# A two-layer encoder trunk: 128-row rotated queries in the attention of layer 0, and the expert selection on 16-bit positions, spread over 55 blocks

## The chip, the cores and the metric

The kernel runs on one core of a Trainium2 chip. The metric is the device time of one execution in microseconds (us); the median of three timed runs of the kernel before is given below. A profiled execution of the same kernel gives the rows.

The engines are TensorE (PE, with its weight loads PEld), VectorE (DVE), ScalarE (ACT), GpSimd (POOL) and SyncE (SP), which issues the DMAs here. Each works through its own instructions in order; semaphores tie them together.

## The reference

256 tokens of width 1024 go through two layers in float32. Each layer is an attention followed by a mixer called PEER, both with a residual and a LayerNorm. The attention of layer 0 is a latent attention: a head's query and key have a content part of 128 and a rotary part of 64, and the rotary key is shared by all heads.

```python
q = einsum('bsr,rhd->bshd', rmsnorm(cq), w_uq)         # 8 heads, 128 + 64
q_nope, q_rope = split(q, [128], axis=-1)
q_rope = apply_rope(q_rope, cos, sin)                  # 64 wide
k_rope = apply_rope(k_rope, cos, sin)                  # one for all heads
q, k = concat([q_nope, q_rope]), concat([k_nope, k_rope])
s = where(key_chunk <= query_chunk, q @ k.T * 192**-0.5, -inf)
o = softmax(s) @ v
```

PEER picks 16 of 16384 experts for each token and head, from two lists of 128 scores:

```python
v1, i1 = top_k(s1, 16);  v2, i2 = top_k(s2, 16)
cand     = v1[..., :, None] + v2[..., None, :]         # 16 x 16 sums
cand_idx = i1[..., :, None] * 128 + i2[..., None, :]   # their experts
best, pos = top_k(cand, 16)
expert = take_along_axis(cand_idx, pos)                # the lookup
gate   = softmax(best)
y = sum over (head, expert) of gelu(x . w_down[expert]) * gate * w_up[expert]
```

## The kernel before

**Weights and products.** All weights come as blocks of 128 x 1024 float32, `raw`, that SP's queue loads in the order of use (`Stream`). ScalarE rounds a block to `hi` (L83) and VectorE makes the rest `lo = raw - hi` (L85); activations are held as such pairs too. `mm3` then does every product as three matmuls, hi by hi, hi by lo and lo by hi (L211). At most three blocks are split ahead of the one in use (`AHEAD`).

**Layer 0's attention.** `mla` makes the normed queries and keys. The rotary queries `qr` hold two heads per tile, head 2i in partitions 0 to 63 and head 2i + 1 in 64 to 127; `rope` writes them with one addition over all 128 partitions (L447). The rotary key `kr` stands twice, in both halves. In `scores` each of two query tiles does a content matmul over 128 rows and a rotary one over 64 (the rows of one head, `qk`, L628 to 630), in float32, followed by mask and maximum on VectorE, the exponential on ScalarE and a division on VectorE. `output` transposes the probabilities (`pt`) and multiplies by the values (`o`). One head's scores are computed ahead of the head whose output is taken.

**PEER.** It doesn't gather. It computes the dot products of all tokens with all 16384 experts and weights them by a mostly empty matrix of gates. First come 16 blocks of queries (`pq`) and the scores (`ps`). Then come 128 blocks of `w_down`: a block is 24 matmuls of 128 x 256 into half a PSUM tile `d`. After each pair of blocks ScalarE applies Gelu and the result is kept in the arena `A`. At last 128 blocks of `w_up` (`y`) multiply `A`.

**The selection.** During the `w_down` blocks the generator `choose` is advanced, `STEPS` calls per block, 2 and 1 alternately. It has 68 steps. For each half of the tokens (t = 0, 1) it first takes the top 16 of each of 16 lists, then forms the 50 sums that can be among the best 16 (`cand`, and on GpSimd their expert numbers `cell`), takes their top 16 with positions `pos`, and looks the numbers up. The lookup of a head is a one-hot and a sum: VectorE compares a counter of 50 cells with the 16 positions (L791, 800 elements a partition, float32, position by position, the cells inmost), GpSimd multiplies by the cells in place (L793), and VectorE adds up over the cells one head later (L796). Behind both halves come the gates, the transposes `gT`, and the split of an expert number into `i1t` and `i2t`.

**Placing.** When the generator has ended (at block 44), 64 groups of four tokens follow. For a token `prepare` makes one-hots of 128 elements in 16-bit floats: `V` on GpSimd (L837), `U` with the gate on VectorE (L838), its rest `L` on ScalarE (L839). `place` multiplies them with eight matmuls into a PSUM tile `G` and folds `G` into `A`. Two groups go with every pair of blocks, and one when fewer than that suffice to end at block 120. The one-hots of two groups are held at a time.

**What sets the order.** The program is written with a tile scheduler: a pass over it with modelled times decides the order of instructions on every engine. So an instruction of the generator need not stand beside the block in whose turn it was written. `STEPS` and the tiles that an instruction needs decide how early it can stand.

Of the kernel before, what the change touches and what calls it, by code (L numbers as in the profile page):

```python
# [12 lines left out]
F16 = mybir.dt.float16  # L13
U32 = mybir.dt.uint32
AF = mybir.ActivationFunctionType
ALU = mybir.AluOpType
AX = mybir.AxisListType

P = 128
T = 256  # L20
# [4 lines left out]
HEADS = 8  # L25
NKEYS = 128
TOPK = 16
# [13 lines left out]
CELLS = sum(SEG)  # L41
STAGGER = 4
STEPS = (2, 1)
FIRST = 4
# [102 lines left out]
def tile_trunk(ctx: ExitStack, tc: tile.TileContext, ins, out: bass.AP):  # L147
    nc = tc.nc
# [3 lines left out]
    const = pool("const", 1)  # L152
# [29 lines left out]
    gr = const.tile([P, T], F32, tag="gr", name="gr")  # L182
    iota16 = const.tile([P, P], F16, tag="iota16", name="iota16")
    arena = big.tile([P, 32768], F32, tag="arena", name="arena")
    A = arena.rearrange("p (b t) -> p b t", t=T)

    make_identity(nc, ident)
    nc.gpsimd.iota(iota, pattern=[[1, P]], base=0, channel_multiplier=0, allow_small_or_imprecise_dtypes=True)
    nc.vector.tensor_copy(iota16, iota)
    nc.vector.memset(ones, 1.0)  # L190
    nc.vector.memset(mhalf, -0.5)
# [243 lines left out]

    def rope(o, p, cos, sin, half, tmp):
        n = p.shape[1]
        xs = tmp()[:, :n, :]
        t1 = tmp()[:, :n, :]
        for q in range(0, P, 2 * half):  # L440
            nc.scalar.copy(xs[q : q + half], p[q + half : q + 2 * half])
            nc.scalar.copy(xs[q + half : q + 2 * half], p[q : q + half])
        cb = cos[:, None, :].to_broadcast([P, n, T])
        sb = sin[:, None, :].to_broadcast([P, n, T])
        nc.vector.tensor_tensor(t1, p, cb, op=ALU.mult)
        nc.gpsimd.tensor_tensor(xs, xs, sb, op=ALU.mult)
        nc.vector.tensor_tensor(o, t1, xs, op=ALU.add)  # L447

# [62 lines left out]
    def mla():  # L511
# [7 lines left out]
        rms = ar.take(2, 2)  # L519
        qn, qr = ar.take(HEADS, T), ar.take(HEADS // 2, T)  # L520
        kn, kr = ar.take(HEADS, T), ar.take(T)
        v = ar.take(2, D)
        oh, ol = xh, xl

        hp = [py(i, f"h{i}") for i in range(3)]
# [73 lines left out]
        for h in range(0, HEADS // 2, 2):  # L599
            p = ps(f"qr{h}")  # L600
            pv = p.rearrange("p (j t) -> p j t", t=T)
            up(pv[:, 0, :], 0, 3)
            up(pv[:, 1, :], 0, 3)
            rope(qr[:, h : h + 2, :], pv, cos, sin, 32, tmp)
        rq = inverse_rms(0, 3, 0)
# [22 lines left out]
        def qk(h):  # L628
            r = slice((h % 2) * 64, (h % 2) * 64 + 64)
            return [(qn[:, h, :], kn[:, h, :]), (qr[r, h // 2, :], kr[r, :])]  # L630

# [84 lines left out]
    def peer(li):  # L716
# [11 lines left out]
        pos = [ar.take(HEADS, TOPK).bitcast(U32) for _ in range(2)]  # L728
        posf = [ar.take(HEADS, TOPK) for _ in range(2)]
        exp_ = [ar.take(HEADS, TOPK) for _ in range(2)]  # L730
        hot = ar.ring(2, TOPK, CELLS)
        scr = ar.ring(2, NKEYS)
        qrow = [arena[:, half - (2 - t) * 512 : half - (1 - t) * 512] for t in range(2)]
# [31 lines left out]
        def choose():  # L765
            for t in range(2):
# [15 lines left out]
                for h in range(HEADS):  # L782
                    top16(best[t][:, h, :], pos[t][:, h, :], cand[t][:, h, :], scr()[:, :CELLS])
                    if h % 2:
                        yield
                nc.vector.tensor_copy(posf[t], pos[t])
                held = None
                for h in range(HEADS + 1):
                    if h < HEADS:
                        o = hot()  # L790
                        nc.vector.tensor_tensor(o, iota[:, None, :CELLS].to_broadcast([P, TOPK, CELLS]),  # L791
                                                posf[t][:, h, :, None].to_broadcast([P, TOPK, CELLS]), op=ALU.is_equal)
                        nc.gpsimd.tensor_tensor(o, o, cell[t][:, h, None, :].to_broadcast([P, TOPK, CELLS]), op=ALU.mult)  # L793
                        yield
# [199 lines left out]
```

## Time and profile before

| | |
|---|---|
| median of 3 runs | 1901.88 us (1901.61 to 1902.59) |
| profiled execution, its span | 1900.2 us, 1898.4 us |
| busy: TensorE, its weight loads | 98%, 88% of the span |
| busy: VectorE, ScalarE, GpSimd | 71%, 56%, 30% of the span |

A row of a group of instructions names its line, engine and operation, then what is written and what is read by the program's names; most tiles of the selection are called `arena`, the big buffer that they are cut from. In a timeline the first number is the start from the beginning of the span and the second the length, both in us. Instructions of one engine overlap at their edges, so the step from one start to the next says more than the length. The granted clock of TensorE, where a view has it, is a share of full speed.

### The profile page before, as it was taken

To read this page: it belongs to the slowest core of one execution; us is meant where nothing else is said; L and a number is where in the kernel's file an instruction comes from. 1 tells how busy PE (TensorE), PEld (TensorE's weight loads), DVE (VectorE), ACT (ScalarE), POOL (GpSimd) and SP (SyncE) were. 2 spreads that over 40 slices of the span, in tenths; PEclk is the share of its full clock that TensorE was granted. 3 is DMA by queue.
4 is the path that set the end of the run, shared out by engine and by line. 5 is a ranking of instruction groups with operands and counts; after the bars stand their busy time and mean duration, and the time that the engine had idled before them with its cause. 6 is when DMAs were issued, how large, how long until landed. Compare 5 with 4: busy or idle time off the path is not lost.

```text
span 1898.4 us, 33300 instructions
## 1 busy us (share of the span) xinstructions
PE 1858.9 (98%) x12482; PEld 1673.4 (88%) x12482; DVE 1356.6 (71%) x2771; ACT 1058.3 (56%) x1837; POOL 565.4 (30%) x648
## 2 busy tenths in 40 slices
PE   8999999999999999999999999999999999999998
PEld 7789999999998888888798799999999988888886
DVE  5579998788766555555668689997887765555555
ACT  6554446777655444444466444558777554444443
POOL 2001346999620000000033003359998400000000
PEclk9999999999999999999999999999999999999999
DMA  6365455444557655555654554554444565555553
GB/s 231 116 217 167 147 176 179 156 156 157 167 172 231 189 189 188 190 188 189 209 167 151 181 160 159 178 189 146 156 157 162 172 228 190 188 191 188 190 187 113
DMA packets 93763, 335.51 MB, mean 177 GB/s; under 512 B 10401, under 2 KB 11425, under 8 KB 93601
## 3 DMA queue, kind: packets, MB, share of 16 engines
q1 hardware_dynamic: 93312, 332.87, 53.3%
q8 instruction: 97, 1.59, 0.3%
q14 instruction: 66, 0.53, 0.1%
q10 hardware_dynamic: 288, 0.52, 0.1%
HBM read 329.16 MB, written 4.19 MB: 176 GB/s over the span
## 4 chain that ended last, share of the span: by engine, by line
PE 85%; DVE 9%; issue 2%; POOL 1%; ACT 1%; DMA 1%; SPq 0%; DVEq 0%; POOLq 0%; ACTq 0%
PE y L211 40%; PE d L211 31%; PE pq L211 4%; PE G L211 3%; DVE lo L85 3%; PE v L211 1%; PE q L211 1%; POOL VU L837 1%; PE s L211 1%; DVE arena L791 1%; DVE arena L796 1%; PE ps L211 1%; PE qw L211 1%; PE qi L211 1%; PE h L211 1%
## 5 line engine op out<-in xcount | busy, mean ns | idle before, releaser
L85 DVE TENSOR_TENSOR lo<-raw,hi 128x1024 fp32r<-128x1024 f32 x587 | 745.4, 1272 | 340.4 <-ACT hi L83 338.6
L83 ACT CAST hi<-raw 128x1024 fp32r<-128x1024 f32 x592 | 619.3, 1048 | 600.1 <-PE y L211 224.3
L211 PE MATMUL d<-xh,lo 128*128 128x256 f32 x2048 | 581.3, 284 | 7.7 <-DVE lo L85 7.7
L211 PE MATMUL d<-xh,hi 128*128 128x256 f32 x2048 | 586.3, 286 | 0.0
L211 PE MATMUL d<-xl,hi 128*128 128x256 f32 x2048 | 579.6, 283 | 0.0
L837 POOL TENSOR_SCALAR VU<-iota,i2t 128x128 f16<-128x128 f16 x512 | 426.4, 850 | 80.7 <-PE G L211 55.5
L211 PEld LDWEIGHTS d<-xh,lo 128*128 128x128 f32 x2048 | 386.8, 189 | 10.5 <-DVE lo L85 10.4
L211 PEld LDWEIGHTS d<-xh,hi 128*128 128x128 f32 x2048 | 387.0, 189 | 0.0
L211 PEld LDWEIGHTS d<-xl,hi 128*128 128x128 f32 x2048 | 387.0, 189 | 0.0
L211 PE MATMUL y<-lo,xh 128*128 128x512 f32 x1088 | 345.1, 395 | 0.0
L211 PE MATMUL y<-hi,xh 128*128 128x512 f32 x1088 | 344.7, 395 | 0.0
L211 PE MATMUL y<-hi,xl 128*128 128x512 f32 x1088 | 344.5, 395 | 0.0
L291 POOL TENSOR_TENSOR st<-st,mhalf 128x1 f32<-128x1 f32 x8 | 4.4, 554 | 864.6 <-DVE st L289 864.6
L211 PEld LDWEIGHTS y<-lo,xh 128*128 128x128 f32 x1088 | 204.8, 188 | 48.0 <-DVE lo L85 0.6
L211 PEld LDWEIGHTS y<-hi,xl 128*128 128x128 f32 x1088 | 205.0, 188 | 47.9
L211 PEld LDWEIGHTS y<-hi,xh 128*128 128x128 f32 x1088 | 204.9, 188 | 47.5
L838 DVE TENSOR_SCALAR VU<-iota,i1t,gt 128x128 f16<-128x128 f16 x512 | 138.5, 344 | 72.5 <-PE G L211 53.9
L839 ACT ACTIVATE U<-VU,gr 128x128 f16<-128x128 f16 x512 | 171.0, 397 | 0.7 <-DVE VU L838 0.4
L893 ACT CAST xh<-arena 128x512 fp32r<-128x512 f32 x128 | 79.2, 620 | 153.1 <-PE y L211 147.8
L894 DVE TENSOR_TENSOR xl<-arena,xh 128x512 fp32r<-128x512 f32 x128 | 88.2, 692 | 80.8 <-ACT xh L893 80.8
L793 POOL TENSOR_TENSOR arena<-arena 128x800 f32<-128x800 f32 x32 | 72.5, 2272 | 96.7 <-DVE arena L791 89.3
L211 PE MATMUL G<-VU 128*128 128x128 f16 x512 | 73.9, 222 | 4.2 <-DVE VU L838 3.0
(222 smaller groups left out, 1853.7 us busy)
## 6 DMA issues: line engine op xcount, KB each, us to landing
raw<-in_down SPq DMA_DIRECT2D x256, 512.0 KB, 3.3
raw<-in_up SPq DMA_DIRECT2D x256, 512.0 KB, 3.3
raw<-in_peer_q SPq DMA_DIRECT2D x32, 512.0 KB, 4.5
raw<-in_dsa_qk SPq DMA_DIRECT2D x16, 512.0 KB, 3.3
raw<-in_mla_w_o SPq DMA_DIRECT2D x8, 512.0 KB, 4.6
raw<-in_dsa_v SPq DMA_DIRECT2D x8, 512.0 KB, 3.4
raw<-in_dsa_w_o SPq DMA_DIRECT2D x8, 512.0 KB, 4.4
raw<-in_mla_qk SPq DMA_DIRECT2D x7, 512.0 KB, 4.6
```

Of the source, the lines that this page charges most:

```text
L83: nc.scalar.copy(hi, raw)
L85: eng.tensor_tensor(lo, raw, hi.bitcast(F32), op=ALU.subtract)
L211: return nc.tensor.matmul(o, l, r, start=start, stop=stop, skip_group_check=True)
L291: nc.gpsimd.tensor_tensor(st[:, 5:6], st[:, 4:5], mhalf, op=ALU.pow)
L791: nc.vector.tensor_tensor(o, iota[:, None, :CELLS].to_broadcast([P, TOPK, CELLS]), posf[t][:, h, :, None].to_broadcast([P, TOPK, CELLS]), ...
L793: nc.gpsimd.tensor_tensor(o, o, cell[t][:, h, None, :].to_broadcast([P, TOPK, CELLS]), op=ALU.mult)
L796: nc.vector.tensor_reduce(exp_[t][:, h - 1, :], held, axis=AX.X, op=ALU.add)
L837: nc.gpsimd.tensor_scalar(V, iota16, i2t[:, t : t + 1], None, op0=ALU.is_equal)
L838: nc.vector.tensor_scalar(U, iota16, i1t[:, t : t + 1], gt[:, t : t + 1], op0=ALU.is_equal, op1=ALU.mult)
L839: nc.scalar.mul(L, U, gr[:, t : t + 1])
L893: nc.scalar.copy(hh, a)
L894: nc.vector.tensor_tensor(al, a, hh.bitcast(F32), op=ALU.subtract)
```

## The change

It has three parts.

The rotary queries get a tile of their own for every head: `qr` grows to one more dimension, and of each head's 128 rows the 64 that belong to the other head are set to zero by GpSimd at the start. `rope` writes the two halves with two additions. The rotary score matmul then uses all 128 rows of `qr` and of `kr`.

The lookup changes its layout. A constant `iotac` holds the cell's number in 16-bit floats, cell by cell with the 16 positions inmost; the positions are cast to 16 bits (`pos16`), and VectorE compares 16-bit with 16-bit into a 16-bit buffer `eq` (two of them, in the tile of the queries, which is no longer needed). GpSimd multiplies those by the float32 cells and writes float32 into the same place as before through a transposed view. It thus goes cell by cell and writes with a step of 50 elements. The sum over cells is unchanged.

`STEPS` becomes 1, 1, 1, 2: five steps in four blocks in place of six. The generator ends at block 54.

```diff
-STEPS = (2, 1)
+STEPS = (1, 1, 1, 2)
...
+    iotac = const.tile([P, CELLS, TOPK], F16, tag="iotac", name="iotac")
...
+    nc.vector.tensor_copy(iotac, iota[:, :CELLS, None].to_broadcast([P, CELLS, TOPK]))
...
-        nc.vector.tensor_tensor(o, t1, xs, op=ALU.add)
+        runs = o if isinstance(o, list) else [(slice(0, P), o)]
+        for r, place in runs:
+            nc.vector.tensor_tensor(place, t1[r], xs[r], op=ALU.add)
...
-        qn, qr = ar.take(HEADS, T), ar.take(HEADS // 2, T)
+        qn, qr = ar.take(HEADS, T), ar.take(HEADS // 2, 2, T)
...
+        halves = [slice(0, 64), slice(64, P)]
+        for i in range(2):
+            nc.gpsimd.memset(qr[halves[1 - i], :, i, :], 0.0)
...
-            rope(qr[:, h : h + 2, :], pv, cos, sin, 32, tmp)
+            rope([(halves[i], qr[halves[i], h : h + 2, i, :]) for i in range(2)], pv, cos, sin, 32, tmp)
...
-            r = slice((h % 2) * 64, (h % 2) * 64 + 64)
-            return [(qn[:, h, :], kn[:, h, :]), (qr[r, h // 2, :], kr[r, :])]
+            return [(qn[:, h, :], kn[:, h, :]), (qr[:, h // 2, h % 2, :], kr)]
...
-        posf = [ar.take(HEADS, TOPK) for _ in range(2)]
+        pos16 = [ar.take(HEADS * TOPK // 2).bitcast(F16).rearrange("p (h k) -> p h k", k=TOPK) for _ in range(2)]
...
+        dead = Arena(qT.rearrange("p a b -> p (a b)"))
+        eq = [dead.take(CELLS * TOPK // 2).bitcast(F16).rearrange("p (c k) -> p c k", k=TOPK) for _ in range(2)]
...
-                nc.vector.tensor_copy(posf[t], pos[t])
+                nc.vector.tensor_copy(pos16[t], pos[t])
...
-                        o = hot()
-                        nc.vector.tensor_tensor(o, iota[:, None, :CELLS].to_broadcast([P, TOPK, CELLS]),
-                                                posf[t][:, h, :, None].to_broadcast([P, TOPK, CELLS]), op=ALU.is_equal)
-                        nc.gpsimd.tensor_tensor(o, o, cell[t][:, h, None, :].to_broadcast([P, TOPK, CELLS]), op=ALU.mult)
+                        o, same = hot(), eq[h % 2]
+                        nc.vector.tensor_tensor(same, iotac, pos16[t][:, h, None, :].to_broadcast([P, CELLS, TOPK]),
+                                                op=ALU.is_equal)
+                        nc.gpsimd.tensor_tensor(o.rearrange("p k c -> p c k"), same,
+                                                cell[t][:, h, :, None].to_broadcast([P, CELLS, TOPK]), op=ALU.mult)
```

The scheduler's order moves with it. On VectorE in layer 0, where the lookups of the second half of the tokens begin, a line before the change is a comparison (L791), a reduction (L796) or a split of a weight block (L85). Before, with the gates of the first half (L805 to L807) among them, these rows stood there:

```order
L791 TENSOR_TENSOR arena_97<-iota_85,arena_97 128x800 x2
L805 TENSOR_REDUCE gs_3317<-arena_97 128x8
L85 TENSOR_TENSOR lo74_2840<-raw74_2729,hi74_2839 128x1024
L806 RECIPROCAL gs_3317<-gs_3317 128x8
L796 TENSOR_REDUCE arena_97<-arena_97 128x16
L807 TENSOR_TENSOR arena_97<-arena_97,gs_3317 128x128
L85 TENSOR_TENSOR lo75_2888<-raw75_2766,hi75_2887 128x1024
L791 TENSOR_TENSOR arena_97<-iota_85,arena_97 128x800
L796 TENSOR_REDUCE arena_97<-arena_97 128x16
L85 TENSOR_TENSOR lo76_2928<-raw76_2806,hi76_2927 128x1024
```

After the change the comparison is L800 and the reduction L806; L815 to L817 belong to the gates of the first half. At the same place stands:

```order
L800 TENSOR_TENSOR arena_98<-iotac_97,arena_98 128x800 x2
L85 TENSOR_TENSOR lo71_2692<-raw71_2581,hi71_2691 128x1024
L815 TENSOR_REDUCE gs_3603<-arena_98 128x8
L806 TENSOR_REDUCE arena_98<-arena_98 128x16
L800 TENSOR_TENSOR arena_98<-iotac_97,arena_98 128x800
L816 RECIPROCAL gs_3603<-gs_3603 128x8
L85 TENSOR_TENSOR lo72_2729<-raw72_2618,hi72_2728 128x1024
L806 TENSOR_REDUCE arena_98<-arena_98 128x16
L800 TENSOR_TENSOR arena_98<-iotac_97,arena_98 128x800
L817 TENSOR_TENSOR arena_98<-arena_98,gs_3603 128x128
L85 TENSOR_TENSOR lo73_2764<-raw73_2660,hi73_2763 128x1024
L806 TENSOR_REDUCE arena_98<-arena_98 128x16
```

Between the second and the third comparison there were two splits and there is one now. From the third on the round was comparison, reduction, split; it is comparison, split, reduction now. The lookups begin three blocks of weights earlier.

On TensorE in layer 0, the first groups of one-hots are placed. A row is a matmul of a block of `w_down` into `d` or one of a group into `G`, or the weight load ahead of it. Before, this stood at group 4:

```order
L211 MATMUL d50_3657<-xl_91,hi90_3544 128x256
L211 MATMUL d50_3657<-xh_90,lo90_3545 128x256
L211 LDWEIGHTS VU_3629
L211 MATMUL G4_3721<-VU_3629 128x128
L211 MATMUL d52_3771<-xh_90,hi91_3574 128x256
L211 MATMUL d52_3771<-xl_91,hi91_3574 128x256
L211 MATMUL d52_3771<-xh_90,lo91_3575 128x256
L211 LDWEIGHTS VU_3629
L211 MATMUL G4_3721<-U_3630,VU_3629 128x128
```

After, the same group stands like this, and line 211 has become 213:

```order
L213 MATMUL d60_3973<-xl_91,hi100_3860 128x256
L213 MATMUL d60_3973<-xh_90,lo100_3861 128x256
L213 LDWEIGHTS VU_3945
L213 MATMUL G4_4037<-VU_3945 128x128
L213 LDWEIGHTS VU_3945
L213 MATMUL G4_4037<-U_3946,VU_3945 128x128
L213 LDWEIGHTS VU_3945
L213 MATMUL G4_4037<-VU_3945 128x128
L213 LDWEIGHTS VU_3945
L213 MATMUL G4_4037<-U_3946,VU_3945 128x128
```

The matmuls of the group, which stood singly among those of `d52`, now stand in one piece behind `d60`. In the eight blocks of the first placing the number of changes between `d` and `G` on TensorE went from 64 to 32.

## Rows read from the trace of the kernel before

**Rows 1.** the page, busy time by engine, and the chain by engine

```profile
PE 1858.9 (98%) x12482; PEld 1673.4 (88%) x12482; DVE 1356.6 (71%) x2771; ACT 1058.3 (56%) x1837; POOL 565.4 (30%) x648
...
PE 85%; DVE 9%; issue 2%; POOL 1%; ACT 1%; DMA 1%; SPq 0%; DVEq 0%; POOLq 0%; ACTq 0%
```

**Rows 2.** stretches: busy us (instructions) by engine, clock, DMA

```profile
53.10:78.10 25.00, 24.74 (x119) 16.53 (x117) 17.26 (x87) 17.37 (x51) 0.00 (x0) 1.00 0.42 158
196.00:232.00 36.00, 34.14 (x279) 33.34 (x278) 36.00 (x61) 16.89 (x19) 15.23 (x7) 1.00 0.46 148
258.00:296.00 38.00, 35.87 (x297) 35.24 (x297) 38.00 (x35) 18.49 (x22) 17.49 (x8) 1.00 0.51 167
```

**Rows 3.** timeline of PE, layer 0 attention: start, length, operation

```profile
68.33 2.06 PE L211 MATMUL s<-arena 128*128 128x128 f32 x8
70.31 0.92 PE L211 MATMUL o<-arena 128*128 128x256 f32 x4
71.07 0.27 PE L477 MATMUL pt<-ident,arena 128*128 128x128 f32 x1
...
74.58 0.82 PE L211 MATMUL o<-arena 128*128 128x256 f32 x4
75.24 0.27 PE L478 MATMUL pt<-ident,arena 128*128 128x128 f32 x1
```

**Rows 4.** timeline of DVE, second half of the selection

```profile
270.59 0.98 DVE L791 TENSOR_TENSOR arena<-iota,arena 128x800 f32<-128x800 f32 x1
271.49 0.97 DVE L796 TENSOR_REDUCE arena<-arena 128x16 f32<-128x800 f32 x1
272.39 2.10 DVE L85 TENSOR_TENSOR lo<-raw,hi 128x1024 fp32r<-128x1024 f32 x1
274.42 0.98 DVE L791 TENSOR_TENSOR arena<-iota,arena 128x800 f32<-128x800 f32 x1
...
282.96 1.21 DVE L85 TENSOR_TENSOR lo<-raw,hi 128x1024 fp32r<-128x1024 f32 x1
```

**Rows 5.** timeline of POOL, one product

```profile
271.65 1.76 POOL L793 TENSOR_TENSOR arena<-arena 128x800 f32<-128x800 f32 x1 [2.06 <-DVE arena L791]
```

**Rows 6.** waits of PE, 260 to 310 us: total, times, longest

```profile
PE d L211 <- DVE lo L85: 2.1, 3, 0.7
```

**Rows 7.** groups of DVE by form, 160 to 320 us: busy, mean ns

```profile
L771 DVE CAST arena<-arena 128x256 f32<-128x256 uint32 x2 | 0.6, 279 | 0.0
...
L786 DVE CAST arena<-arena 128x128 f32<-128x128 uint32 x2 | 0.4, 222 | 0.0
```

**Rows 8.** groups of POOL by form, 160 to 330 us

```profile
L778 POOL TENSOR_TENSOR arena<-arena 128x16 f32<-128x16 f32 x6 | 1.2, 229 | 0.0
L778 POOL TENSOR_TENSOR arena<-arena 128x64 f32<-128x64 f32 x2 | 0.6, 306 | 0.0
```

**Rows 9.** timeline of POOL, one 16-bit one-hot alone

```profile
519.44 0.59 POOL L837 TENSOR_SCALAR VU<-iota,i2t 128x128 f16<-128x128 f16 x1
```

**Rows 10.** groups of POOL, 336 to 470 us

```profile
L837 POOL TENSOR_SCALAR VU<-iota,i2t 128x128 f16<-128x128 f16 x159 | 132.8, 852 | 1.7 <-PE G L211 1.1
```

**Rows 11.** timeline of PE, placing and dots interleaved

```profile
310.27 0.36 PE L211 MATMUL d<-xh,hi 128*128 128x256 f32 x1
310.47 0.23 PE L211 MATMUL G<-U,VU 128*128 128x128 f16 x1
```

**Rows 12.** chain of waits, 300 to 380 us: start, length, what

```profile
305.51 0.77 PE d L211 x6
...
336.83 5.74 PE d L211 x48
342.57 0.91 PE G L211 x16
...
363.56 5.74 PE d L211 x48
...
377.22 2.78 PE d L211 x23
```


## The prediction, made before the changed kernel was run

> **What bounds the kernel now.** I read the page's busy times and its chain first: TensorE works 98% of the span and carries 85% of the chain, VectorE 9% [rows 1]. An edit therefore pays only where it shortens TensorE's own instructions or removes a stretch in which TensorE stands still. I then went by stretches, at a full granted clock throughout [rows 2]. In layer 0's attention TensorE is busy 24.74 of 25.00 us while VectorE has 17.26 and ScalarE 17.37, so there the length of its matmuls counts. In the two halves of the selection VectorE is busy the whole stretch, and TensorE gets 279 and 297 matmuls of 0.12 us done, which is 33.5 of 36 and 35.6 of 38 us: 2.5 and 2.4 us lost per half. The waits of TensorE say for what: `lo`, three times, up to 0.7 us [rows 6]. Last I read the chain over the onset of placing [rows 12] and GpSimd's one-hots behind it [rows 10].
>
> **A. 128-row queries.** A head's scores (two query tiles, content part and rotary part) take from 68.33 to 70.31, 1.98 us, and the `o` product behind them 0.76 to the next start, where another `o` with nothing of the sort ahead takes 0.66 [rows 3]. `o` streams 384 columns in four passes; the scores stream 768, so at the pace of `o` they would take 2 x 0.66 = 1.32. The 64-row rotary matmuls and the changes of row count around them thus cost 0.66 + 0.10 = 0.76 per head, 8 x 0.76 = 6.1 us. With full rows all of it can go. Next in line is ScalarE with 17.4 us: at a stretch of 20 it would be at 87% [rows 2], close enough that a little will be waited for. Bounds -6.1 and 0 (all hidden behind the softmax); I take -5.0, near the row.
> The additions to this part I cost at nothing. Two more rope additions, each at most half of a 1.21 us subtraction [rows 4], stand before TensorE's `kn` products, which cover them; uncovered +1.2. The two memsets are GpSimd's, at the start; the constant's cast lies on VectorE before the first input has landed, and would cost at most one 0.97 us pass [rows 4].
>
> **B. The selection on 16-bit positions.** Per head VectorE does is_equal 0.90, the reduction 0.90 and one `lo` to the next is_equal 2.03 [rows 4]: 3.83 us, while TensorE eats a block (24 matmuls) in 2.88. `lo` alone is 1.21 long [rows 4]; beside GpSimd's product, which is 1.76 long and waited for VectorE 2.06 [rows 5], it is 2.10. So product, is_equal and `lo` go in turn: 1.76 + 0.90 + 1.17 = 3.83. Over eight heads VectorE falls 8 x 0.95 = 7.6 us behind and TensorE loses 2.4: the `lo` made ahead cover the other 5.2.
> The new is_equal has two 16-bit inputs and a 16-bit result, which no row has. Bounds: unchanged (0.98 long); and the slope of casts, (279 - 222)/128 = 0.45 ns an element [rows 7], which for 800 with the same start-up gives 0.52 long, about 0.45 to the next start. I take 0.45: the operands are dense in memory, like the cast's. That takes 8 x 0.45 = 3.6 us from each half. Against it stands the new order: where two `lo` stood between the second and the third is_equal of a half there is one now, so the blocks made ahead are fewer by one step of a `lo`, 2.0 us [rows 4], when the row of heads begins. The order shows it in the second half; I charge it in each. Behind by 7.6 - 3.6 + 2.0 = 6.0, less the cover of 5.2, leaves 0.8 lost of 2.4; I take 1.2, half of what is lost now, because VectorE stays without a gap in the stretch: -1.2 per half, four halves, -4.8. Best case, no loss left, -9.8; at an unchanged is_equal the 2.0 is paid in every half, +8.0.
> (The Trainium skill, VectorE: DVE Perf Modes, in its section on the modes, lets a two-input operation do two elements a cycle when every tensor is 16 bits wide and dense, at 0.96 GHz. No run here shows it yet. By it is_equal would be an estimated 800/1.92 = 0.42 us plus its start, and the sum would stay.)
> The product itself changes: it reads 16-bit flags beside 32-bit cells and writes 32-bit results at a step of 200 bytes. I keep 1.76. No row has that form; the nearest are the last in rows 8 and 9, used under the first rival. Nothing speaks for a cheaper one, so this bound is one-sided.
>
> **C. Where placing begins.** The generator now ends at block 54, not 44, and the first group is placed at 58, not 48. The order shows 64 alternations between `d` and `G` in the eight blocks of onset before, 32 now. From 305.51 to 336.83 the eight blocks take 31.3 us [rows 12]; their matmuls are 8 x 2.88 + 10 groups x 0.46 = 27.6 (a pair of groups takes 0.91 [rows 12]), so 3.7 are lost. A `d` matmul beside a `G` has its successor 0.20 later, not 0.12 [rows 11]: 64 x 0.08 = 5.1 at most, and 32 fewer give 2.6 a layer. Bounds 0 and -2.6; the remaining loss comes from first one-hots that aren't ready, which stays. I take -1.5 a layer: -3.0.
>
> **D. A later end of the two-group pairs.** After the onset two groups go with every pair of blocks. GpSimd makes eight one-hots a pair, 8 x 0.852 = 6.82 us [rows 10], and the chain shows (377.22 - 363.56)/2 = 6.83 us per pair, where TensorE needs 5.75 + 0.91 = 6.66 [rows 12]: 0.17 lost in each of the sixteen pairs of blocks 64 to 95. The four pairs before them lose nothing (336.83 to 363.56 is 26.7 us, four times 6.66 is 26.6 [rows 12]): GpSimd had got ahead while the onset lost its 3.7 us. By the code's rule 26 pairs get two groups now, 31 after the change, up to block 118. Four fall on the onset; with less lost there I give the next ones no credit, so 27 pairs run at that pace, 11 more: 1.9 a layer, +3.8. Bounds 0 (the buffers absorb it) and +5.1, 15 pairs more.
>
> **Sum.** -5.0 - 4.8 - 3.0 + 3.8 = -9.0. The profiled execution took 1900.2 us (span 1898.4); with -9.0 it is 1891.2. The median of the timed runs stands 1.7 above the profiled one: **1893 us**. SP's queue keeps its weight stream; two small loads change places in it, at nothing.
>
> **Rivals.**
> R1, slower: GpSimd's product gets dearer with 16-bit input and strided writes. For it: GpSimd's 32-bit two-input slope is (306 - 229)/48 = 1.6 ns an element [rows 8], so 128 elements would be 0.41, but a 16-bit one-hot of 128 takes 0.59 [rows 9]; 0.18 more for 128 is 1.4 ns an element, 1.1 us on 800. Against it: that one-hot is another operation with a scalar in memory. The product stands in the cycle that `lo` waits for, so 8 x 1.1 = 8.8 us are added to each half: 0.8 + 8.8 = 9.6 lost instead of 2.4, +29 in four halves, and -5.0 + 29 - 3.0 + 3.8 = +25: 1927. It decides from a product longer than 1.76 by (4.2/4 + 1.2)/8 = 0.28, about 2.04 us.
> (The Trainium skill, GPSIMD Engine Reference, section 7 on pitfalls, charges reads whose step exceeds 8 bytes 2.9 cycles an element instead of 1.9. It speaks of reads; here the writes have the step, and no row shows a strided write. If writes paid alike, an estimate of half more than 1.76 would be 2.64, and R1 would hold.)
> R2: is_equal is no faster at 16 bits. Then B is +8.0, the sum -5.0 + 8.0 - 3.0 + 3.8 = +3.8: 1906. The positions are broadcast over the cells in runs of 16, which may keep the engine at its old pace; the casts of rows 7 have one input only.
> R3: the scores' saving hides behind the softmax and the transposes that wait for it, A = 0: 1898. For it: `pt` waits for ScalarE and VectorE each head. Against it: they have 30% of the stretch free [rows 2].
>
> **How the numbers follow.** Forecast 0.60, its own range 1886 to 1899 (A full and B best against R3's half); R1 0.18, R2 0.10, R3 0.12. Range 1885 to 1912: it leaves out about half of R1's weight and little below. A measurement here tells about 0.2%, 3.8 us, from no change: faster is below 1898.1, slower above 1905.7. Forecast gives 0.55 faster and 0.05 same; R3 half faster; R2 half same, half slower; R1 0.16 slower and 0.02 same. Together faster 0.61, same 0.18, slower 0.21.
>
> **What would show it.** A: score rows all of 128x128, 1.3 to 1.4 us per head, and the `y` products of out_proj starting 5 us earlier. B: is_equal near 0.5 and the product near 1.76 in its row, TensorE's waits for `lo` below 1 us. C: the matmuls of a group in one piece at a pair's end. D: the 6.83 pace up to block 118. The forecast is wrong if the product is above 2 us, or if attention isn't shorter.

## The result, and the profile after

The changed kernel takes 1878.53 us (median of four runs, 1878.0 to 1879.34) against 1901.92: a ratio of 0.9876, 95% interval 0.9864 to 0.9888, or -23.4 us. The forecast was -9.0 and 1893, its range ended at 1885. The profiled execution has a span of 1876.7 us, 21.7 below that of before. By stages these 21.7 are: the attention of layer 0, from its first score to the first `y`, -6.1, and what lies ahead of it +0.8; the `w_down` blocks -7.5 and -8.2; the `pq` blocks -0.5 and -1.5; the attention of layer 1 -1.5; the `w_up` blocks +1.5 each.

The attention gave what the forecast had set as its bound. The timeline of TensorE, at a head's scores (start us, length us, operation):

```profile
66.86 1.48 PE L213 MATMUL s<-arena 128*128 128x128 f32 x8
68.17 0.82 PE L213 MATMUL o<-arena 128*128 128x256 f32 x4
68.82 0.27 PE L482 MATMUL pt<-ident,arena 128*128 128x128 f32 x1
```

The scores take 1.31 us from start to start where [rows 3] had 1.98, and the `o` behind them 0.65 instead of 0.76. I had worked out 1.32 and 0.66. The stage begins with a head's scores amid the last `v` products and ends at the first `y`. Before:

```profile
53.13 0.80 PE L211 MATMUL s<-arena 128*128 128x128 f32 x4
...
78.09 0.48 PE L211 MATMUL y<-hi,xh 128*128 128x512 f32 x1
```

After:

```profile
53.89 0.61 PE L213 MATMUL s<-arena 128*128 128x128 f32 x4
...
72.77 0.48 PE L213 MATMUL y<-hi,xh 128*128 128x512 f32 x1
```

It lasts 18.88 us where it lasted 24.96, 6.1 less. The first `y` comes only 5.3 earlier, because this execution reached its first score 0.8 later. That isn't the change's doing as far as the runs show: in the versions of the changed kernel below it comes between 52.2 and 53.1, and in the kernel before at 53.13.

The lookup, on VectorE in the second half of the selection:

```profile
250.31 0.97 DVE L806 TENSOR_REDUCE arena<-arena 128x16 f32<-128x800 f32 x1
251.21 1.06 DVE L800 TENSOR_TENSOR arena<-iotac,arena 128x800 f16<-128x800 f16 x1
252.19 1.21 DVE L85 TENSOR_TENSOR lo<-raw,hi 128x1024 fp32r<-128x1024 f32 x1
253.33 0.97 DVE L806 TENSOR_REDUCE arena<-arena 128x16 f32<-128x800 f32 x1
```

and in the first half, where small operations of the other half's lists (left out here) lie between `lo` and the next reduction:

```profile
203.21 0.97 DVE L806 TENSOR_REDUCE arena<-arena 128x16 f32<-128x800 f32 x1
204.10 0.56 DVE L800 TENSOR_TENSOR arena<-iotac,arena 128x800 f16<-128x800 f16 x1
204.59 1.21 DVE L85 TENSOR_TENSOR lo<-raw,hi 128x1024 fp32r<-128x1024 f32 x1
...
206.19 0.96 DVE L806 TENSOR_REDUCE arena<-arena 128x16 f32<-128x800 f32 x1
```

with the product on GpSimd, one that waits for a `lo` and the last, which doesn't (in brackets how long GpSimd was idle before, and for what):

```profile
252.41 2.58 POOL L802 TENSOR_TENSOR arena<-arena 128x800 f32<-128x800 f16 x1 [0.44 <-DVE arena L800]
...
261.46 1.71 POOL L802 TENSOR_TENSOR arena<-arena 128x800 f32<-128x800 f16 x1 [0.42 <-DVE arena L800]
```

Undisturbed the comparison is 0.56 us long, where [rows 4] had 0.98. In the second half a round lasts from 250.31 to 253.33, 3.02 us, where [rows 4] had 3.83. `lo` is at its bare 1.21, not 2.10: now it is the product that waits for `lo`, and the comparison (1.06 long, so 0.50 of it waiting) for the product. In the first half the small operations fill that half microsecond, and nothing on VectorE waits. TensorE's waits from 155 to 290 us, over both halves, have shrunk to one (total, times, longest), where before they were 4.0 us in six:

```profile
PE d L213 <- DVE lo L85: 0.6, 1, 0.6
```

What no term of mine foresaw shows where nothing waits. Two stretches, one of `d` in layer 0, ahead of TensorE's first wait there, and one of `y`: length, TensorE busy (matmuls), granted clock, DMA. Before:

```profile
172.00:196.00 24.00, 24.00 (x202) 1.00 0.56 176
600.00:860.00 260.00, 260.00 (x1121) 1.00 0.59 190
```

After:

```profile
172.00:196.00 24.00, 24.00 (x206) 1.00 0.51 172
600.00:860.00 260.00, 260.00 (x1116) 1.00 0.56 188
```

The same clock, the same matmuls, TensorE busy throughout, and yet four more of `d` in 24 us and five fewer of `y` in 260. From start to start, four blocks of `d` (96 matmuls) take 11.31 us wherever nothing waits, where before they took 11.52 in some stretches and 11.39 in others; a `y` takes 233.3 ns where it took 232.4.

### The profile page after: what moved, and what is told of

The parts are those of the page before. It is cut to its first block, busy times and chain, and to the rows that moved or that the text cites. A ratio compares the mean times of both kernels' runs of the same rounds, so it can differ in the third digit from the quotient of the medians.

```text
span 1876.7 us, 33300 instructions
## 1 busy us (share of the span) xinstructions
PE 1840.9 (98%) x12482; PEld 1655.3 (88%) x12482; DVE 1326.3 (71%) x2764; ACT 1052.4 (56%) x1827; POOL 577.9 (31%) x650
## 5 line engine op out<-in xcount | busy, mean ns | idle before, releaser
L85 DVE TENSOR_TENSOR lo<-raw,hi 128x1024 fp32r<-128x1024 f32 x587 | 725.6, 1238 | 365.7 <-ACT hi L83 364.6
L213 PE MATMUL d<-xh,hi 128*128 128x256 f32 x2048 | 579.4, 283 | 0.0
L213 PE MATMUL d<-xh,lo 128*128 128x256 f32 x2048 | 572.8, 280 | 0.9 <-DVE lo L85 0.9
L213 PE MATMUL d<-xl,hi 128*128 128x256 f32 x2048 | 572.9, 280 | 0.0
L847 POOL TENSOR_SCALAR VU<-iota,i2t 128x128 f16<-128x128 f16 x512 | 430.8, 859 | 112.1 <-DVE i2t L836 100.5
L802 POOL TENSOR_TENSOR arena<-arena 128x800 f32<-128x800 f16 x32 | 79.0, 2488 | 41.0 <-DVE arena L800 40.1
```

What stands on the lines that cost most here:

```text
L85: eng.tensor_tensor(lo, raw, hi.bitcast(F32), op=ALU.subtract)
L213: return nc.tensor.matmul(o, l, r, start=start, stop=stop, skip_group_check=True)
L802: nc.gpsimd.tensor_tensor(o.rearrange("p k c -> p c k"), same, cell[t][:, h, :, None].to_broadcast([P, CELLS, TOPK]), op=ALU.mult)
L847: nc.gpsimd.tensor_scalar(V, iota16, i2t[:, t : t + 1], None, op0=ALU.is_equal)
```

## The experiments

All times are medians, beside runs of the kernel before on the same chip. The theory after the result: TensorE's pace hangs on where its operands lie, and the new constant (1600 bytes a partition) moved them. Its rival: on the phase of events. The next four runs also take the parts of the change one by one.

**The place alone.** The kernel before, and:

```diff
+    pad = const.tile([P, CELLS, TOPK], F16, tag="pad", name="pad")
     arena = big.tile([P, 32768], F32, tag="arena", name="arena")
...
```

Expected: 

> The kernel before with one more tile of 1600 bytes a partition among the constants, set to zero once and read by nobody; all buffers allocated behind the constants move by 1600 bytes. Theory P (TensorE's pace depends on where the buffers lie; the new constant moved them): the d matmuls step at 117.8 ns instead of 118.7 to 120, the pq matmuls at 119.9 instead of 123.4 on average, the y matmuls at 233.5 instead of 232.6; about -4 to -10 us from d, -3 from pq, +3 from y: 1892 to 1898 us. Rival Q (the pace hangs on the order and the phase of the events, not on the place): steps as before, 1901 to 1903 us.

Measured: 1897.51 us against 1902.1, ratio 0.9979 (0.9969 to 0.9988). The two stretches have the changed kernel's counts:

```profile
172.00:196.00 24.00, 24.00 (x206) 1.00 0.56 176
600.00:860.00 260.00, 260.00 (x1116) 1.00 0.57 189
```

Four `d` blocks take 11.31 us, a `y` 233.3 ns. An unread tile is worth -4.6 us; the rival is out. In the selection TensorE, now faster, loses more than before: blocks 16 to 23 take 26.3 us where 22.6 would do, 3.7 lost. In the kernel before the same blocks took 25.8 where 23.0 would have done, 2.8 lost.

**128-row queries alone.**

```diff
-            return [(qn[:, h, :], kn[:, h, :]), (qr[r, h // 2, :], kr[r, :])]
+            return [(qn[:, h, :], kn[:, h, :]), (qr[:, h // 2, h % 2, :], kr)]
...
```

Expected: 

> Only the 128-row rotated queries. The first y matmul of layer 0 came 5.3 us earlier with the whole change; if that is this part's, here too: 1896 to 1897 us with every other stage as before. Theory P expects the d and y steps of before; rival Q allows other steps, since all later events move by 5 us.

Measured: 1894.6 us, ratio 0.9966 (0.9956 to 0.9977), -7.5 with an interval from -8.4 to -4.4. From the first score to the first `y` it takes 18.88 us as in the changed kernel, -6.1; `d` and `y` step as before, though every later event comes some 6 us earlier, which speaks against the rival once more.

**The lookup alone** (with `iotac`, and so with the place).

```diff
-                        nc.vector.tensor_tensor(o, iota[:, None, :CELLS].to_broadcast([P, TOPK, CELLS]),
+                        nc.vector.tensor_tensor(same, iotac, pos16[t][:, h, None, :].to_broadcast([P, CELLS, TOPK]),
...
```

Expected: 

> Only the lookup on 16-bit positions with its constant, the generator at 2, 1 steps a block as before. My prediction's term B is -4.8 us; theory P adds its -4 to -6 us of pace, since the constant is here: 1889 to 1893 us with d steps of 117.8 ns. Rival Q: 1896 to 1898 us with d steps of 119 to 120. The loss of 2.4 us per half should fall to 1.2 or below.

Measured: 1885.73 us, ratio 0.9915 (0.9899 to 0.9932): -16.4, more than expected. Against the place alone it is -11.8; the `d` stages are 6.3 and 6.5 us shorter than with the place alone, -12.8 together. Blocks 16 to 23 lose nothing any more, and 36 to 43 lose 0.7 us in layer 0.

**The steps alone.**

```diff
-STEPS = (2, 1)
+STEPS = (1, 1, 1, 2)
```

Expected: 

> Only the steps 1, 1, 1, 2. My terms C and D give +0.8 us together: 1902 to 1903 us. A rival, that the spreading by itself relieves VectorE in the selection, gives a loss of about 0 in both halves of the old lookup, -10 us: 1892 us. d steps as before by both theories of the pace.

Measured: 1901.62 us, ratio 0.9997 (0.9988 to 1.0007), no change. Both terms are there. In layer 0, blocks 44 to 63 take 63.8 us instead of 69.9 and hold 80 matmuls of groups fewer (4.6 us at 0.46 per eight), a gain of 1.5; blocks 64 to 127 take 214.0 instead of 207.5 and hold these 80 more, a loss of 1.9. In layer 1 the gain is 1.5 and the loss 1.4.

**Which move counts.** Three versions of the kernel before, each with 64 bytes: behind the constants, ahead of `xh`, and ahead of `hi`. The last one's edit:

```diff
     raws = pool("raws", 4)
+    padp = pool("padp", 1)
     his = pool("his", 4)
...
+    pad = padp.tile([P, 16], F32, tag="pad", name="pad")
...
```

Expected behind the constants: 

> The kernel before with a tile of 64 bytes a partition, set to zero and not read, behind the constants: the arena, the weight buffers raw, hi, lo and the rest move by 64 bytes; xh and xl stay. 1600 is 64 more than a multiple of 512. Theory P1 (the position within 128 bytes decides TensorE's pace): as with the 1600 bytes, four d blocks in 11.31 us, y at 233.5 ns, 1896 to 1899 us. Rival P2 (how far apart the buffers lie, or which large region of the memory they touch): d as before, 11.39 to 11.52 us, 1901 to 1903 us.

Expected ahead of everything: 

> The same 64 bytes, but ahead of xh and xl, so that these move too and all products' operands keep their distances. Theory P1a (the absolute position of the weight operand in 128 bytes): d in 11.31 us for four blocks, and y, whose weights are xh and xl, changes as well, below 232.6 ns. Theory P1b (the distance between the operands): d 11.39 to 11.52 us, y 232.6 ns, 1901 to 1903 us.

Expected with `hi` and `lo` alone: 

> The 64 bytes between raw and hi: only hi and lo move, by 64 bytes. If the pace is set by TensorE's own reads of hi and lo against xh and xl: d 11.31 us for four blocks, y 233.5 ns, as with the pad behind the constants. If it is set by the arena, by raw or by the DMAs' writes there: d 11.39 to 11.52 us.

Measured: 1896.64 us (0.9977, 0.9967 to 0.9988); 1900.59 (0.9997, 0.9987 to 1.0007); 1898.9 (0.9986, 0.9977 to 0.9996). The first and the third have `d` at 11.31 us and `y` at 233.3 ns, the second `d` at 11.39 to 11.52 and `y` at 232.4 as before, in its stretches:

```profile
172.00:196.00 24.00, 24.00 (x203) 1.00 0.52 172
600.00:860.00 260.00, 260.00 (x1120) 1.00 0.57 190
```

So 64 bytes do what 1600 do, and it is the distance between `hi`, `lo` and `xh`, `xl` that counts: moving all of them changes nothing. The arena, `raw` and its DMAs have no part in it.

**The comparison in float32, all else as changed.**

```diff
-        pos16 = [ar.take(HEADS * TOPK // 2).bitcast(F16).rearrange("p (h k) -> p h k", k=TOPK) for _ in range(2)]
+        pos16 = [ar.take(HEADS, TOPK) for _ in range(2)]
...
-        eq = [dead.take(CELLS * TOPK // 2).bitcast(F16).rearrange("p (c k) -> p c k", k=TOPK) for _ in range(2)]
+        eq = [dead.take(CELLS, TOPK) for _ in range(2)]
+        iotac = dead.take(CELLS, TOPK)
...
```

Expected: 

> The changed kernel with the comparison in float32: counter, positions and flags are 32 bits wide, with the layout, the separate buffer for the flags, the transposed writing and all addresses of buffers kept; one more pass of 0.9 us per layer fills the counter. Theory O (the comparison takes 0.45 us more, but product's start stays hidden behind the lo): cycle 3.01 + 0.42 = 3.43 us, behind by 8 x 0.6 = 4.8 us per half, of which the blocks ahead cover 4 to 5: 1879 to 1883 us. Rival S (the 16-bit comparison carries the gain): cycle back at 3.83, 3 to 4 us lost per half, 1890 to 1893 us.

Measured: 1890.42 us, ratio 0.9934 (0.9918 to 0.9951), where the rival put it. My own figure, 1879 to 1883, was wrong: the scheduler knows that this comparison is slower and made another order, with two reductions and two splits in a row, so that the round I had counted on isn't repeated. It stands there once, in the second half:

```profile
275.31 0.97 DVE L809 TENSOR_REDUCE arena<-arena 128x16 f32<-128x800 f32 x1
276.21 1.49 DVE L803 TENSOR_TENSOR arena<-arena 128x800 f32<-128x800 f32 x1
277.62 1.21 DVE L85 TENSOR_TENSOR lo<-raw,hi 128x1024 fp32r<-128x1024 f32 x1
278.75 0.97 DVE L809 TENSOR_REDUCE arena<-arena 128x16 f32<-128x800 f32 x1
```

That is 3.44 us with the new order and the old comparison, between the 3.83 of before and the 3.02 of the changed kernel. Where nothing holds it up, this comparison is 0.97 us long.

**16 bits in the old layout.** Flags position by position, the positions read with step 0, the product written without a step.

```diff
-                        nc.vector.tensor_tensor(same, iotac, pos16[t][:, h, None, :].to_broadcast([P, CELLS, TOPK]),
+                        nc.vector.tensor_tensor(same, iota16[:, None, :CELLS].to_broadcast([P, TOPK, CELLS]),
+                                                pos16[t][:, h, :, None].to_broadcast([P, TOPK, CELLS]),
...
```

Expected: 

> The changed kernel with the lookup on 16 bits, but in the old layout: flags position by position with the cells inmost, so that the positions are read with step 0 and GpSimd writes without a step. All addresses and the flags' own buffers are kept. If the comparison's speed needs the positions inmost: is_equal 0.98 us again, and the loss of the 32-bit comparison, 1888 to 1892 us. Rival (16 bits alone do it): is_equal 0.56 us, 1877 to 1880 us. In both the product, without the step of 200 bytes, shows what the step costs; I expect 1.7 us, as with it.

Measured: 1891.94 us, ratio 0.9951 (0.9934 to 0.9968). The first half has rounds with the same operations as the changed kernel's first half above, on VectorE:

```profile
203.41 0.96 DVE L806 TENSOR_REDUCE arena<-arena 128x16 f32<-128x800 f32 x1
204.29 1.03 DVE L800 TENSOR_TENSOR arena<-iota,arena 128x800 f16<-128x800 f16 x1
205.24 1.22 DVE L85 TENSOR_TENSOR lo<-raw,hi 128x1024 fp32r<-128x1024 f32 x1
...
206.90 0.97 DVE L806 TENSOR_REDUCE arena<-arena 128x16 f32<-128x800 f32 x1
```

Later on stand an undisturbed comparison, and one round in the order of the changed kernel's second half:

```profile
254.82 0.98 DVE L800 TENSOR_TENSOR arena<-iota,arena 128x800 f16<-128x800 f16 x1
...
273.40 0.97 DVE L806 TENSOR_REDUCE arena<-arena 128x16 f32<-128x800 f32 x1
274.30 1.55 DVE L800 TENSOR_TENSOR arena<-iota,arena 128x800 f16<-128x800 f16 x1
275.77 1.21 DVE L85 TENSOR_TENSOR lo<-raw,hi 128x1024 fp32r<-128x1024 f32 x1
276.91 0.97 DVE L806 TENSOR_REDUCE arena<-arena 128x16 f32<-128x800 f32 x1
```

and on GpSimd a product that waits for nothing:

```profile
255.94 1.66 POOL L803 TENSOR_TENSOR arena<-arena 128x800 f32<-128x800 f16 x1 [3.02 <-DVE gs L816]
```

The round is 206.90 - 203.41 = 3.49 us, in the changed kernel 206.19 - 203.21 = 2.98: the dense comparison saves 0.51 a round, and the kernel without it is 13.4 us slower, about what the whole lookup had gained. Not all of the 13.4 is the comparison itself, since in the second half the scheduler made another order here too. 16 bits alone give nothing. The product with the step of 200 bytes is 1.71 - 1.66 = 0.05 us longer; the order in which it reads the cells differs as well.

**32 bytes more.** The changed kernel with `hi` and `lo` moved by 32 bytes, as above.

Expected: 

> The changed kernel with hi and lo 32 bytes further, everything else in place. In the kernel before hi and xh lay at the same place in 128 bytes (both 64), in the changed one 64 apart. If only whole steps of 64 bytes matter: d and y as in the changed kernel (11.31 us for four blocks, 233.5 ns), 1877 to 1880 us. If the two streams' meeting in 64-byte pieces matters: another pace, from 10.88 (the fastest seen, in eight blocks after the 64 bytes) to 11.52: 1864 to 1890 us.

Measured: 1876.14 us, ratio 0.9871 (0.9854 to 0.9887). `d` goes to 11.20 us (11.31 from block 40 on), `y` stays at 233.3 ns: less than 64 bytes matter.

**One one-hot in eight on VectorE**, in the changed kernel, to test the term D.

```diff
-                nc.gpsimd.tensor_scalar(V, iota16, i2t[:, t : t + 1], None, op0=ALU.is_equal)
+                eng = nc.vector if t % 8 == 7 else nc.gpsimd
+                eng.tensor_scalar(V, iota16, i2t[:, t : t + 1], None, op0=ALU.is_equal)
```

Expected: 

> The changed kernel with every eighth one-hot V written by VectorE instead of GpSimd, one per pair of blocks with two groups. My term D says that such a pair waits for GpSimd, 8 x 0.852 = 6.82 us; with seven it needs 6.0, less than TensorE's 6.63. The four-block stretches from block 64 to 119, now 13.5 to 13.7 us, should take 13.27 to 13.35: about 3 to 4 us less per layer, 1870 to 1873 us. Rival (VectorE, which has 27 to 28 other operations in a pair, becomes the bound, or blocks GpSimd): no change or slower, 1878 to 1884 us.

Measured: 1866.95 us, ratio 0.9819 (0.9802 to 0.9835), 11.6 below the changed kernel and more than expected. The one-hots of the stretch from 350 to 470 us, in the changed kernel (busy us, mean ns, idle before them and for what):

```profile
L847 POOL TENSOR_SCALAR VU<-iota,i2t 128x128 f16<-128x128 f16 x142 | 119.8, 861 | 1.4 <-PE G L213 1.0
```

and here:

```profile
L848 POOL TENSOR_SCALAR VU<-iota,i2t 128x128 f16<-128x128 f16 x128 | 94.3, 753 | 26.9 <-PE G L213 26.9
...
L848 DVE TENSOR_SCALAR VU<-iota,i2t 128x128 f16<-128x128 f16 x18 | 4.5, 248 | 0.0
```

GpSimd, without a gap before, now waits for TensorE, and four blocks take 13.24 us from block 64 to 115, instead of 13.47 to 13.7.

**The old steps in the changed kernel.**

```diff
-STEPS = (1, 1, 1, 2)
+STEPS = (2, 1)
```

Expected: 

> The changed kernel with the steps 2, 1 of before: what the spreading is worth in the company of the rest. My terms C and D say +0.3 per layer for the spreading alone, which is what it showed alone (no change): 1877 to 1880 us. Rival (with the selection no longer late, the spreading relieves the second half or the onset): 1882 us or more without it.

Measured: 1879.99 us (1878.93 to 1880.52), ratio 0.9884 (0.9867 to 0.99). That is 1.5 us above the changed kernel, within the two intervals: the spreading is worth nothing that these runs can tell.

**Which distance.** Two versions of the kernel before, with `hi` and `lo` moved by 128 and by 32 bytes, and the changed kernel with the shared one-hots and 32 bytes.

Expected with 128: 

> The kernel before with hi and lo 128 bytes further. If TensorE's pace goes by the distance between the operands within 128 bytes: as before, four d blocks in 11.39 to 11.52 us, y 232.6 ns, 1900 to 1903 us. If any other distance than the old one helps: 11.31 us, 1896 to 1899 us.

Expected with 32: 

> The kernel before with hi and lo 32 bytes further, half of the shift that gave 11.31 us. If 32 bytes are as good as 96 (which the changed kernel with 32 more has): 11.20 us, 1894 to 1898 us. If it lies half way between 0 and 64: 11.4 us, 1897 to 1901 us.

Expected of the combination: 

> The changed kernel with every eighth V on VectorE and hi and lo 32 bytes further. If the two gains add up (-11.6 us for the sharing, -2.4 for the place, against 1878.5): 1863 to 1866 us. If the faster d blocks make VectorE late again in the second half of the selection (12.83 instead of 12.14 us with the 32 bytes alone), less: 1866 to 1869 us.

Measured: 1885.83 us (0.9921, 0.9904 to 0.9937), 1909.81 (1.0051, 1.0033 to 1.0069), and 1861.97 (0.9789, 0.9772 to 0.9805), the last 1 us below its range. The first two expectations were wrong, and with them the idea that only the place within 128 bytes counts. With 128 bytes `d` is at 11.52 us, the slow one of the paces before, but `y` runs as it did nowhere else:

```profile
172.00:196.00 24.00, 24.00 (x202) 1.00 0.55 176
600.00:860.00 260.00, 260.00 (x1149) 1.00 0.62 195
```

With 32 bytes `y` is the slowest seen, 234.3 ns. The two products want different distances, and at 128 bytes `y` weighs more: it gains 5.7 ns in each of 3264 matmuls, 18.6 us, while `d` loses some 3.

**A distance for each product.** In the version with the shared one-hots, `xh` and `xl` are seen at two places of one tile; `y`'s operands go to the one, all others to the other. `hi` and `lo` are moved as well, so that `y` comes to distance 0 each time. The edit of the first one, without that pad:

```diff
+    xx = const.tile([P, 2 * NC * T + 8], F32R, tag="xx", name="xx")
+    pair = lambda at: [xx[:, at + i * NC * T : at + (i + 1) * NC * T].rearrange("p (c t) -> p c t", t=T) for i in range(2)]
+    xh, xl = pair(8)
+    yh, yl = pair(0)
...
-                hh, al = xh[:, slot, :], xl[:, slot, :]
+                hh, al = yh[:, slot, :], yl[:, slot, :]
```

Expected with 480 bytes for `d`: 

> The changed kernel with every eighth V on VectorE, and with xh and xl seen at two places of one tile, 32 bytes apart: the d products (and all others) use the one at 480 bytes, modulo 512, from hi and lo, the y products the one at 0. If the pace is a matter of the distance between a product's two operands: d in 11.20 us as at 480, y at 227.0 ns as with the 128 bytes, 10 us less per layer than the version with 32 bytes, 1841 to 1846 us. If it is the place of hi and lo alone, y stays at 233.5 ns and the time at 1862 us, or d goes to 11.52 us.

Expected with 256: 

> The same with 256 bytes between the two views: y at distance 0, d at 256, which no run had. d in four blocks anywhere from 10.9 to 11.6 us; y at 227.0 ns if the distance counts. 1840 to 1856 us.

Expected with 128: 

> The same with 128 bytes between the views: y at distance 0, d at 128, which no run had. d in four blocks anywhere from 10.9 to 11.6 us; y at 227.0 ns if the distance counts. 1840 to 1856 us.

Measured: 1844.24 us (0.9692, 0.9675 to 0.9708), 1858.0 (0.9768, 0.9752 to 0.9785; 2 us above its range) and 1853.18 (0.9743, 0.9727 to 0.9759). The first one's two stretches:

```profile
172.00:196.00 24.00, 24.00 (x208) 1.00 0.55 179
600.00:860.00 260.00, 260.00 (x1149) 1.00 0.59 193
```

Both products have their best pace in one kernel, so the distance between a product's own two operands sets it. This version is 34 us faster than the changed kernel; 22.7 of them are the distances (1866.95 to 1844.24), the rest the shared one-hots. All distances that ran (address of `hi` minus that of the tile it meets, modulo 512; the addresses are those of the built programs):

| distance, bytes | 0 | 128 | 256 | 384 (before) | 416 | 448 (changed) | 480 |
|---|---|---|---|---|---|---|---|
| four blocks of `d`, us | 11.52 | 11.39 to 11.52 | 11.52 | 11.39 to 11.52 | 11.52 | 11.31 (10.88 after some waits) | 11.20 to 11.31 |
| one `y`, ns | 226.7 | | | 232.4 | 234.3 | 233.3 | 233.3 |

## Why the prediction was wrong

The direction was right and the size was not: -23.4 us for -9.0, outside the range. By its own terms:

| term | forecast, us | measured, us | from |
|---|---|---|---|
| A, scores | -5.0 | -6.1 | the attention stage, alone and with the rest |
| B, lookup | -4.8 | -12.8 | the `d` stages of the lookup alone against the place alone |
| C, onset | -3.0 | -3.1 | both layers, the steps alone |
| D, GpSimd's pairs | +3.8 | +3.2 | both layers, the steps alone |
| the place of the buffers | none | -4.6 | the unread tile |
| sum | -9.0 | -23.4 | |

The measured sum is that of the medians (23.4); the spans differ by 21.7. Terms read from single traces are good to about 1 us (the `pq` blocks of layer 1 took 41.7 us before and 40.7 with the 128-row queries alone), so the close agreement is partly luck. Of the 14.4 us that the forecast missed, B has 8.0, the place 4.6 and A 1.1.

**The constant cost nothing, I said, and looked at its cast alone.** That step failed: a term put at nothing measured -4.6. The price of a new tile was not in the instruction that fills it: it pushed `hi` and `lo` 64 bytes (1600 is 3 x 512 + 64) against `xh` and `xl`, and every `d` and `y` matmul changed pace. No instruction was added to TensorE, no wait, and the clock was the same. The trace of before did have a sign of it that I passed over: four undisturbed blocks took 11.52 us in one stretch and 11.39 in another, and I took 2.88 us a block for a constant of the machine.

**B was the largest miss, and its charge for the order had the wrong sign.** I put the comparison at 0.45 us less a head, and the two layouts differ by 0.51. I then added 2.0 us per half because one `lo` fewer stood ahead of the third comparison, and rounded the remaining loss up to 1.2. Neither showed: the first half loses nothing, the second some 0.7. Nor did the +8.0 that I gave the new order with an unchanged comparison: the float32 run, which has the place and the 128-row queries too, takes 1890.42 us, and 1902 - 4.6 - 6.1 is 1891. In the second half the round shrank by 0.81 (3.83 to 3.02), so 0.3 to 0.4 more than the comparison accounts for. In the rows, `lo` now runs between a comparison and the next reduction, while the product made from that comparison is waiting; before, `lo` came after the reduction and had to wait out the rest of the product, 0.89 of its 2.10. What waits now is the comparison, and only 0.50. Two single rounds with the new order and the old comparison agree: 3.44 us in the float32 run, and 3.51 with 16 bits in the old layout (from 273.40 to 276.91 there). So 0.3 to 0.4 of the 0.81 is the order and the rest the comparison, on these two rounds; no run has eight of them in a row, since the scheduler then chose another order. With rounds of 3.02 against a TensorE block of 2.83, VectorE falls behind by 8 x 0.19 = 1.5 us a half, less than the 5.2 that I had the blocks ahead cover; what the second half still loses, this count doesn't explain. The rest of the term's size comes from the place: beside a faster TensorE the old lookup loses 3.7 us in the first half and not 2.8, so there was more to win.

**A, C and D held.** A reached its bound of -6.1; the 1.1 that I had left for waits on the softmax wasn't needed. C and D cancel; the steps alone show no change, and alone was the only way to see both. For D the run with the shared one-hots shows the cause as well. That the fewer changes between `d` and `G` made C, as I had argued, no run shows by itself.

**The rivals.** R1 needed a product above 2.04 us; it is 1.71 alone. The Trainium skill (GPSIMD Engine Reference, section 7) charges strided reads; the product with the stepped write is 0.05 us longer here, so the rule doesn't carry over to this write. R2 did not hold: 0.56 for 0.98 us. The Trainium skill (VectorE: DVE Perf Modes, section Mode 2×_1P) asks for 16-bit tensors and a step of one for two elements a cycle. The runs bear out both conditions: 0.56 us with both met, 0.97 in the same layout in float32, and 0.98 in 16 bits with one operand at step 0. R3 did not hold: the attention shrank by the 6.1 us counted for TensorE.

What stays open: why the distance acts. The pace is known at seven distances for `d` and at five for `y`; whether it repeats every 256 bytes (128 as 384, 0 as 256 for `d`) or every 512 isn't settled, nor why one kernel holds 11.39 and 11.52 us at one distance.

## What to carry to other kernels

When an engine is the bound at 98%, look at its step from start to start in undisturbed stretches before any wait: 2% there weighs more than a stall. Whoever adds a tile should compare the addresses of the bounding engine's operands before and after, and try pads of 32 to 128 bytes on purpose, each measured: 128 bytes gained 16 us here and 32 lost 8. Where two products share an operand, they can want different distances. When the rows show two engines holding each other up, as `lo` (2.10 us for 1.21) and the product (2.58 for 1.71) do here, count the round of all of them by what is queued behind what, and not the busy time of each.

## What the runs showed that I had not expected

- The distance between a matmul's two operands in memory sets its step: a `y` from 226.7 to 234.3 ns, a block of `d` from 2.80 to 2.88 us, the whole kernel from 1885.83 to 1909.81 us by a pad of 128 or of 32 bytes alone.
- After some waits `d` ran faster for a while: with the 64 or the 1600 bytes behind the constants, four blocks took 10.88 us in blocks 24 to 31 of layer 1. Nothing tried here brings that about at will.
- VectorE writes the one-hot of 128 in 0.25 us, GpSimd in 0.75 to 0.86. One in eight moved away took TensorE's wait for the other seven with it.
